# A hybrid decoder layer with retrieved experts: the first half's gates, merge and scores by two tiles at a time, and larger runs of the expert tables

## The chip, the core and the metric

The kernel runs on one core of one Trainium2 chip. The core has a matrix engine (TensorE, PE in the profile; its weight loads are PEld), a vector engine (VectorE, DVE), a scalar engine (ScalarE, ACT), GpSimd (POOL), which also issues the gathers, and SyncE (SP), which issues most other DMAs. All DMAs of the core run on 16 DMA engines. The metric is the device time of the launch in microseconds. Before the change it is 3426.83 us, the median of three executions.

## The reference

The layer takes `x` (1024 tokens of 1024 channels, float32). With `u` the normalised input it computes

```python
proj = u @ w_in                  # b_gate, c_gate, xc, q, k, v, g_conv, g_attn
y_conv = (b_gate * conv3(c_gate * xc)) @ w_conv_out
y_attn = merge3(dilated_window_attention(q, k, v)) @ w_attn_out    # 24 heads, 3 dilations
merged = sigmoid(g_conv + b0) * y_conv + sigmoid(g_attn + b1) * y_attn
h = x + merged @ w_out
u2 = rms_norm(h)
q = u2 @ w_query                 # 8 heads x 2 halves of 128
s = q . sub_keys                 # 128 scores for each half of each head
idx, gates = best 16 of the 256 sums of the top 16 of both halves
a = gelu(u2 . expert_down[idx])  # 8 x 16 = 128 of 16384 experts for each token
out = rms_norm(h + sum((gates * a) * expert_up[idx]))
```

The mixing is causal: the second half of the tokens reads keys, values and the convolution's carry of the first half.

## The kernel before

The tokens are two halves of 512, and tiles of 128. Matrix products run in fp32r with both sides split into a high and a low part, three matmuls for each pair of blocks (`mm3`, L175 to L178). `weights` (L161) loads 512 KB of a weight, casts the high part on ScalarE (L165) and subtracts it on DVE (L167, "a weight split" below); four buffers hold raw weights, two hold the split ones. `project` (L184) makes 24 matmuls from one weight and a block of activations, whose token columns are the moving side.

`mixer(half)` (L354) makes the projections, attention and convolution of a half, then its end: `gates` (L604; 16 projections and sigmoids), `merge` (L616; 8 products with `w_attn_out`, 8 with `w_conv_out`, each multiplied with its gate), `product` (L663; `w_out`, two columns halves, and the residual) and `tail` (L694; second norm, transposes, 16 projections with `w_query`, and the scores). The pair `SUBS[half]` says how the four tiles of a half are cut: the first number how many groups go through gates and merge, the second into how many parts a group is cut for product and tail. The first half has (1, 2): all four tiles through gates and merge with 512 columns, then product and tail for tiles 0 and 1, and for 2 and 3. While a tail waits for its norm, `AFTER` steps of what comes next are put ahead of it (L698).

The experts are computed in two ways. For tiles of the first half, `choose` (L756) finds the 16 best experts of each head on DVE, and `experts` (L861) gathers the rows of the chosen experts, 128 for each token, one row for each of the tile's 128 tokens at a time: POOL issues the gather of a 128x1024 block into one of four buffers, and DVE multiplies and sums it (L875, 512 times) or adds it into the result (L891, 384 times). For the second half and for tile 1's up products, `dense` (L900) goes through all 16384 experts: `hidden` (L909) computes gelu of the down products, 128 projections, `build` (L948) makes a table of gates by one-hot products (`g_d` in HBM), and then 32 steps follow. A step loads the stored hidden units (`fetch`, L920), reads its part of the table (`gg`, L984), multiplies and splits (`weigh`, L983), and runs 120 matmuls against the rows of `up` (L1063), whose splits are `uh` and `ul`. `STORED` = 27 of the 32 blocks of hidden units go through HBM; four (`HOLD`) stay in buffers, and one is computed within the loop (L1041).

What sets the order: each engine takes its instructions in one order that is fixed when the kernel is built. The builder's scheduler sees the instructions in the order of the program, in which the generators are interleaved by paces (`PACE_B`, `PACE_C`, `PACE_D`, L1108 to L1120), and may move a later one ahead when it takes an engine to be idle and the instruction ready. The experts' generator stands behind the first half in the program (L1103 to L1105). The pool of ten big buffers (`BIGS`, 16 KB of each partition) holds most activations, `gg`, `ga`, `hh` and `hl`.

Of the kernel before, what the change touches and what calls it, by code (L numbers as in the profile page):

```python
# [8 lines left out]
F32 = mybir.dt.float32  # L9
# [4 lines left out]
ALU = mybir.AluOpType  # L14
# [22 lines left out]
RATE_G = 0.8  # L37
STORED = 27
HOLD = 4
RAWS = 4  # L40
HILO = 2
SUBS = ((1, 2), (1, 1))
OBUF = 4
# [22 lines left out]
def hybrid_layer(ctx, tc, x, xT, pos, rotc, norm_mix, w_proj, w_v, conv_w, w_conv_out, w_attn_out,  # L66
                 gate_bias, w_out, norm_ffn, w_query, sub_keys, down, down_t, up, final_norm, out):
    nc = tc.nc
# [111 lines left out]
    def split(hi, lo, src):  # L180
        S.copy(hi, src)  # L181
        V.tensor_tensor(lo, src, hi.bitcast(F32), op=ALU.subtract)  # L182
# [717 lines left out]
    def dense():  # L900
# [47 lines left out]
        def build(srcs, c0):  # L948
# [5 lines left out]
                for c in range(c0, c0 + P // TC):  # L954
# [25 lines left out]
                    for w in range(4):  # L980
                        nc.sync.dma_start(g_d[c, :, 32 * w:32 * w + 32], stg[w])

        def weigh(q):  # L983
            gg = m8.tile([P, TH // TC, NB, TC], F32, tag="big", name="gg")  # L984
            nc.sync.dma_start(gg, g_d[:TH // TC, :, NB * q:NB * q + NB].rearrange("c j i t -> j c i t"))
            ga = gas.pop(q)
            hh, hl = bigr("hh"), bigr("hl")
            for ii in range(NB):
                v = ga[:, ii].rearrange("p (c t) -> p c t", t=TC)
                V.tensor_tensor(v, v, gg[:, :, ii], op=ALU.mult)  # L990
                split(hh[:, ii], hl[:, ii], ga[:, ii])
            parts = [(hh[:, :, tt * P:tt * P + P], hl[:, :, tt * P:tt * P + P]) for tt in range(4)]
# [41 lines left out]
        for n_q, q in enumerate(order):  # L1034
# [22 lines left out]
            for n in range(2):  # L1057
                uu = []
                whole = [bigr("uh_end"), bigr("ul_end")] if end and n else None
                for ii in range(0, NB, 2):  # L1060
                    raw = wp.tile([P, 2, TH], F32, tag="raw", bufs=RAWS, name="rawu")
                    r0 = (NB * q + ii) * P
                    nc.sync.dma_start(raw, up[r0:r0 + 2 * P, n * TH:n * TH + TH].rearrange("(a p) d -> p a d", a=2))  # L1063
                    if whole:
                        uh, ul = (t[:, ii:ii + 2] for t in whole)
                    else:
                        uh = up_p.tile([P, 2, TH], F32R, tag="uu", bufs=UPS, name="uh")
                        ul = up_p.tile([P, 2, TH], F32R, tag="uu", bufs=UPS, name="ul")
                    split(uh, ul, raw)
                    uu.append((uh, ul))  # L1070
# [105 lines left out]
```

## Time and profile before

| | |
|---|---|
| median of three executions | 3426.83 us (3426.28 to 3431.36) |
| the profiled execution | 3433.88 us |
| its span, first to last instruction | 3432.1 us |
| mean granted clock of TensorE | 0.984 |
| busy: TensorE, DVE, ScalarE, POOL | 3274.4, 2760.1, 1461.7, 1190.2 us |
| DMA | 948.08 MB, 276 GB/s in the mean |

A stretch of time is read by the engines' busy time in it: the one that is busy all the time sets its length, and where two are, the order in which each takes its work decides. Matmuls are pipelined, so the mean duration of one in a group is longer than the distance from one to the next; that distance is a stretch's time over its count. Small float32 products that aren't split (scores, transposes, table) show as two matmuls each.

### The profile page before, as it was taken

Reading aid. Unit: us, or ns where it says so; the run is one execution under the profiler, and the core shown is the slowest. Engines: PE = TensorE matmul, PEld = TensorE weight load, DVE = VectorE, ACT = ScalarE, POOL = GpSimd, SP = SyncE. Lnnn points to the kernel's source line nnn. Section 1 sums busy time; section 2 is a strip of 40 time slices with the busy share of each in tenths; the row PEclk is TensorE's granted clock in tenths of the full one; section 3 lists DMA queues with packets and bytes.
Section 4 is the critical chain, followed back from the end, with each engine's and each line's share of the span. In section 5 each row is a group of like instructions: output and inputs, shape, how many; then the busy total and the mean of one; then the engine's idle time right before and its main releaser. Section 6 shows DMA issues by size and latency. Waiting matters only on the chain.

```text
span 3432.1 us, 47074 instructions
## 1 busy us (share of the span) xinstructions
PE 3274.4 (95%) x15923; PEld 2685.0 (78%) x15923; DVE 2760.1 (80%) x5646; ACT 1461.7 (43%) x3271; POOL 1190.2 (35%) x944
## 2 busy tenths in 40 slices
PE   7999999999989999988999989999999999999998
PEld 6787888887767777767777878888877878787787
DVE  4333355689999889988999999998887878888887
ACT  3544444443334353333226777787632222222222
POOL 0000000014543345555434443464544334444342
PEclk9999999999989999989999999999999999999999
DMA  4233335668888678988889898999989989999895
GB/s 129 77 119 110 103 127 191 244 230 305 302 279 276 227 260 307 342 316 292 315 316 328 329 330 334 344 340 336 348 301 336 334 316 338 326 340 333 309 350 208
DMA packets 364307, 948.08 MB, mean 276 GB/s; under 512 B 33952, under 2 KB 127648, under 8 KB 356640
## 3 DMA queue, kind: packets, MB, share of 16 engines
q1 hardware_dynamic: 232016, 465.27, 38.9%
q0 software_dynamic: 132048, 479.78, 38.8%
q8 instruction: 126, 2.06, 0.2%
q14 instruction: 117, 0.96, 0.1%
HBM read 843.15 MB, written 95.49 MB: 273 GB/s over the span
## 4 chain that ended last, share of the span: by engine, by line
PE 32%; DVE 20%; DMA 14%; issue 11%; POOL 5%; ACT 1%; SPq 0%; DVEq 0%; POOLq 0%; ACTq 0%
DVE row L875 6%; PE ps L178 6%; PE ps L176 6%; PE ps L177 6%; DMA row<-in_down,idx 5%; DMA rowu<-in_up,idx 4%; DMA gg<-g_d 4%; DVE lo L167 3%; POOL row L873 3%; POOL rowu L889 2%; PE held L177 2%; PE held L178 2%; PE held L176 2%; DVE acc L891 1%; PE psg L975 1%
## 5 line engine op out<-in xcount | busy, mean ns | idle before, releaser
L873 POOL DMA_INDIRECT row<-in_down,idx x512 | 640.9, 1252 | 885.2 <-DVE a L875 465.6
L889 POOL DMA_INDIRECT rowu<-in_up,idx x384 | 525.8, 1369 | 621.1 <-DVE acc L891 499.0
L165 ACT CAST hi<-raw 128x1024 fp32r<-128x1024 f32 x368 | 387.6, 1053 | 746.0 <-PE ps L177 541.1
L875 DVE CUSTOM_DVE_ANT_0 row<-row,ut 128x1024 f32<-128x1024 f32 x512 | 618.8, 1215 | 79.2 <-DMA row<-in_down,idx 74.0
L167 DVE TENSOR_TENSOR lo<-raw,hi 128x1024 fp32r<-128x1024 f32 x368 | 448.1, 1218 | 247.9 <-ACT hi L165 238.6
L178 PE MATMUL ps<-vhi,lo 128*128 128x512 f32 (+1 forms) x1408 | 535.4, 382 | 33.5 <-DVE lo L167 33.4
L176 PE MATMUL ps<-vhi,hi 128*128 128x512 f32 (+1 forms) x1408 | 530.6, 377 | 10.8 <-ACT hi L165 6.7
L891 DVE SCALAR_TENSOR_TENSOR acc<-rowu,a,acc 128x1024 f32<-128x1024 f32 x384 | 491.2, 1279 | 59.7 <-DMA rowu<-in_up,idx 57.3
L177 PE MATMUL ps<-vlo,hi 128*128 128x512 f32 (+1 forms) x1408 | 528.9, 376 | 0.0
L178 PE MATMUL ps<-uhi,lo 128*128 128x512 f32 x1024 | 409.1, 400 | 4.2 <-DVE lo L167 4.2
L176 PE MATMUL ps<-uhi,hi 128*128 128x512 f32 x1024 | 407.6, 399 | 5.7 <-ACT uhi L181 3.1
L177 PE MATMUL ps<-ulo,hi 128*128 128x512 f32 x1024 | 409.1, 400 | 0.5 <-DVE ulo L182 0.5
L178 PEld LDWEIGHTS ps<-vhi,lo 128*128 128x128 f32 x1408 | 269.1, 191 | 87.4 <-DVE lo L167 44.4
L176 PEld LDWEIGHTS ps<-vhi,hi 128*128 128x128 f32 x1408 | 269.7, 192 | 58.9 <-ACT hi L165 10.9
L177 PEld LDWEIGHTS ps<-vlo,hi 128*128 128x128 f32 x1408 | 269.1, 191 | 45.1
L177 PE MATMUL held<-ul,hh 128*128 128x512 f32 x624 | 247.0, 396 | 11.1 <-DVE ul L182 10.9
L178 PE MATMUL held<-uh,hl 128*128 128x512 f32 x624 | 244.0, 392 | 2.5 <-DVE hl L182 2.5
L176 PEld LDWEIGHTS ps<-uhi,hi 128*128 128x128 f32 x1024 | 194.1, 190 | 52.1 <-ACT uhi L181 5.2
L176 PE MATMUL held<-uh,hh 128*128 128x512 f32 x624 | 233.3, 393 | 0.0
L178 PEld LDWEIGHTS ps<-uhi,lo 128*128 128x128 f32 x1024 | 194.3, 190 | 47.9 <-DVE lo L167 6.4
L177 PEld LDWEIGHTS ps<-ulo,hi 128*128 128x128 f32 x1024 | 194.1, 190 | 45.1 <-issue 3.0
L181 ACT CAST hh<-ga 128x512 fp32r<-128x512 f32 x128 | 71.4, 618 | 353.0 <-DVE ga L990 348.9
(347 smaller groups left out, 5947.8 us busy)
## 6 DMA issues: line engine op xcount, KB each, us to landing
raw<-in_w_proj SPq DMA_DIRECT2D x128, 512.0 KB
raw<-in_down_t SPq DMA_DIRECT2D x128, 512.0 KB
rawu<-in_up SPq DMA_DIRECT2D x128, 512.0 KB
g_d<-stg SPq DMA_DIRECT2D x80, 512.0 KB
gg<-g_d SPq DMA_DIRECT2D x32, 1024.0 KB
a_d<-ga SPq DMA_DIRECT2D x27, 1024.0 KB
ga<-a_d SPq DMA_DIRECT2D x27, 1024.0 KB
raw<-in_w_query SPq DMA_DIRECT2D x48, 512.0 KB
```

Of the source, the lines that this page charges most:

```text
L165: S.copy(hi, raw)
L167: V.tensor_tensor(lo, raw, hi.bitcast(F32), op=ALU.subtract)
L176: PE.matmul(ps, l[0], r[0], start=first, stop=False)
L177: PE.matmul(ps, l[0], r[1], start=False, stop=False)
L178: PE.matmul(ps, l[1], r[0], start=False, stop=last)
L181: S.copy(hi, src)
L873: G.indirect_dma_start(out=row, out_offset=None, in_=down, in_offset=bass.IndirectOffsetOnAxis(ap=idx[:, e:e + 1], axis=0))
L875: V.tensor_tensor_reduce(out=row, in0=row, in1=ut, scale=1.0, scalar=0.0, op0=ALU.mult, op1=ALU.add, accum_out=a[:, e:e + 1])
L889: G.indirect_dma_start(out=row, out_offset=None, in_=up, in_offset=bass.IndirectOffsetOnAxis(ap=idx[:, e:e + 1], axis=0))
L891: V.scalar_tensor_tensor(acc, row, a[:, e:e + 1], acc, op0=ALU.mult, op1=ALU.add)
L975: PE.matmul(ps[:, t], ob[:, t], oa[:, t], start=True, stop=True)
```

## The change

In the first half, `SUBS` becomes (2, 1): tiles 0 and 1 go through gates, merge, product and tail, then tiles 2 and 3. Gates and merge so run on 256 columns, and twice. Four gate projections of the second group stand ahead of the first tail, where the second product stood.

`weigh` reads the table for two steps at once: at an even step two transfers bring half of the tokens each, in runs of 1 KB where there were runs of 512 B, and both stay for the odd step. It multiplies and splits in pieces of 128x1024. For the pairs to be whole, `STORED` is 28, and no hidden block is computed within the loop. The rows of `up` come from a copy that is laid out ahead of the launch, so that each partition reads one run of 4 KB where it read two of 2 KB.

```diff
-STORED = 27
+STORED = 28
...
-SUBS = ((1, 2), (1, 1))
+SUBS = ((2, 1), (1, 1))
...
+        pairs = {}
+
         def weigh(q):
-            gg = m8.tile([P, TH // TC, NB, TC], F32, tag="big", name="gg")
-            nc.sync.dma_start(gg, g_d[:TH // TC, :, NB * q:NB * q + NB].rearrange("c j i t -> j c i t"))
+
+            c2 = TH // TC // 2
+            if q // 2 not in pairs:
+                both = []
+                for half in range(2):
+                    gg = m8.tile([P, c2, 2 * NB, TC], F32, tag="big", name="gg")
+                    i0 = 2 * NB * (q // 2)
+                    nc.sync.dma_start(gg, g_d[c2 * half:c2 * half + c2, :, i0:i0 + 2 * NB].rearrange("c j i t -> j c i t"))
+                    both.append(gg)
+                pairs[q // 2] = both
+            gg2 = pairs[q // 2]
             ga = gas.pop(q)
             hh, hl = bigr("hh"), bigr("hl")
-            for ii in range(NB):
-                v = ga[:, ii].rearrange("p (c t) -> p c t", t=TC)
-                V.tensor_tensor(v, v, gg[:, :, ii], op=ALU.mult)
-                split(hh[:, ii], hl[:, ii], ga[:, ii])
+            for half in range(2):
+                cols = slice(half * TH // 2, half * TH // 2 + TH // 2)
+                v = ga[:, :, cols]
+                g = gg2[half][:, :, NB * (q % 2):NB * (q % 2) + NB].rearrange("p c i t -> p i c t")
+                V.tensor_tensor(v.rearrange("p i (c t) -> p i c t", t=TC), v.rearrange("p i (c t) -> p i c t", t=TC), g,
+                                op=ALU.mult)
+                split(hh[:, :, cols], hl[:, :, cols], v)
...
-                    r0 = (NB * q + ii) * P
-                    nc.sync.dma_start(raw, up[r0:r0 + 2 * P, n * TH:n * TH + TH].rearrange("(a p) d -> p a d", a=2))
+                    nc.sync.dma_start(raw, up_s[(NB * q + ii) // 2, n])
...
+        "up_s": i["peer_up"][0].reshape(P // 2, 2, P, 2, TH).transpose(0, 3, 2, 1, 4),
```

The order of instructions changes with it. The first place is DVE's order where the first gathered rows stand. Before, they stand in the second tail, between the splits of `w_query`; the choice of tile 0 ends with L828, and L762 to L766 choose for tile 1:

```order
L826 SCALAR_TENSOR_TENSOR e_5667<-e_5667 128x128
L828 CAST idx<-e_5667 128x128
L762 MAX tv<-sv 128x8 x4
L763 MAX_INDEX ti<-tv,sv 128x8 x2
L167 TENSOR_TENSOR lo<-raw,hi 128x1024
L763 MAX_INDEX ti<-tv,sv 128x8 x2
L764 MATCH_REPLACE sv<-tv,sv 128x128 x4
L765 MAX tv<-sv 128x8 x2
L875 ISA row,a<-row,ut 128x1024
L875 ISA a 128x1
L765 MAX tv<-sv 128x8
L167 TENSOR_TENSOR lo<-raw,hi 128x1024
```

After, on the same engine, they stand in the merge of tiles 2 and 3, between the splits of `w_conv_out`; L631 multiplies the gate with the attention product, L649 with that of the convolution:

```order
L167 TENSOR_TENSOR lo<-raw,hi 128x1024
L631 TENSOR_TENSOR sg_4701<-sg_4701,ya 128x256
L764 MATCH_REPLACE sv<-tv,sv 128x128 x3
L875 ISA row,a<-row,ut 128x1024
L875 ISA a 128x1
L765 MAX tv<-sv 128x8 x4
L875 ISA row,a<-row,ut 128x1024
L875 ISA a 128x1
L167 TENSOR_TENSOR lo<-raw,hi 128x1024
L649 TENSOR_TENSOR sg_5868<-sg_5868,ys 128x256
L766 MAX_INDEX ti<-tv,sv 128x8 x4
L875 ISA row,a<-row,ut 128x1024
```

The row products have moved ahead of a merge's end, a product and a tail of the first half.

The second place is SP's order in the steps of `dense`, two steps of each kernel. Before, a step fetches `ga` and its table `gg`, then goes on with the rows of `up` (`rawu`) and tile 1's part of the table (`gx`):

```order
L922 DMA ga<-a_d 128x2048
L985 DMA gg<-g_d 128x16x128
L1063 DMA rawu<-in_up 128x2x512
L996 DMA gx<-g_d 128x4x128
L1063 DMA rawu<-in_up 128x2x512 x3
L922 DMA ga<-a_d 128x2048
L985 DMA gg<-g_d 128x16x128
L1063 DMA rawu<-in_up 128x2x512
L996 DMA gx<-g_d 128x4x128
L1063 DMA rawu<-in_up 128x2x512 x3
```

After, the two parts of a pair's table stand on both sides of three loads of `up`:

```order
L922 DMA ga<-a_d 128x2048
L1076 DMA rawu<-in_up_s 128x1024
L1010 DMA gx<-g_d 128x4x128
L922 DMA ga<-a_d 128x2048
L993 DMA gg<-g_d 128x8x256
L1076 DMA rawu<-in_up_s 128x1024 x3
L993 DMA gg<-g_d 128x8x256
L1076 DMA rawu<-in_up_s 128x1024
L1010 DMA gx<-g_d 128x4x128
L1076 DMA rawu<-in_up_s 128x1024 x3
```

The odd step has no table to read; the even step's second part is issued behind loads that wait for a raw buffer.

## Rows read from the trace of the kernel before

**Rows 1.** The page: busy us of each engine, and tenths in 40 slices.
```profile
PE 3274.4 (95%) x15923; PEld 2685.0 (78%) x15923; DVE 2760.1 (80%) x5646; ACT 1461.7 (43%) x3271; POOL 1190.2 (35%) x944
...
PE   7999999999989999988999989999999999999998
...
DVE  4333355689999889988999999998887878888887
```

**Rows 2.** Stretches: us, busy PE, PEld, DVE, ACT, POOL, clock, DMA share, GB/s.
```profile
500.00:628.00 128.00, 126.62 (x551) 102.53 (x551) 76.67 (x110) 65.33 (x90) 0.68 (x1) 1.00 0.59 202
628.00:776.00 148.00, 138.44 (x952) 127.30 (x952) 123.81 (x389) 68.48 (x139) 17.96 (x17) 0.95 0.68 237
776.00:1057.00 281.00, 258.09 (x1325) 207.54 (x1323) 267.48 (x851) 100.49 (x200) 133.63 (x121) 0.94 0.87 295
1057.00:1609.00 552.00, 517.68 (x2535) 417.43 (x2534) 484.02 (x964) 217.16 (x414) 254.35 (x203) 0.97 0.83 288
1609.00:1924.00 315.00, 292.79 (x1362) 238.02 (x1362) 302.61 (x853) 142.72 (x349) 134.74 (x112) 0.99 0.89 319
1924.00:2461.00 537.00, 521.05 (x2787) 446.45 (x2787) 506.48 (x955) 405.17 (x1281) 252.83 (x173) 0.98 0.91 336
2461.00:3432.00 971.00, 939.71 (x4067) 762.20 (x4066) 793.30 (x1049) 246.15 (x352) 394.06 (x307) 0.99 0.89 319
```

**Rows 3.** The same view: 512-column work alone, then mostly 256-column work.
```profile
560.00:595.00 35.00, 35.00 (x156) 29.01 (x155) 20.86 (x28) 13.54 (x19) 0.00 (x0) 1.00 0.31 103
655.00:690.00 35.00, 35.00 (x298) 35.00 (x297) 29.67 (x94) 17.34 (x44) 1.08 (x2) 1.00 0.65 209
```

**Rows 4.** Groups on DVE, 628 to 776 us: count, busy us, mean ns, idle before.
```profile
L167 DVE TENSOR_TENSOR lo<-raw,hi 128x1024 fp32r<-128x1024 f32 x36 | 43.9, 1219 | 15.0 <-ACT hi L165 14.9
L875 DVE CUSTOM_DVE_ANT_0 row<-row,ut 128x1024 f32<-128x1024 f32 x8 | 9.7, 1221 | 2.2 <-DMA row<-in_down,idx 2.1
L182 DVE TENSOR_TENSOR vlo<-pst,vhi 128x256 fp32r<-128x256 f32 x16 | 6.3, 416 | 0.3 <-ACT vhi L181 0.2
...
L765 DVE MAX8 tv<-s_t 128x8 f32<-128x128 f32 x16 | 4.6, 290 | 0.4
```

**Rows 5.** Groups of the whole span, by form.
```profile
L875 DVE CUSTOM_DVE_ANT_0 row<-row,ut 128x1024 f32<-128x1024 f32 x512 | 618.8, 1215 | 79.2 <-DMA row<-in_down,idx 74.0 <-issue 4.0 <-DMA ut<-u_d 0.9
...
L891 DVE SCALAR_TENSOR_TENSOR acc<-rowu,a,acc 128x1024 f32<-128x1024 f32 x384 | 491.2, 1279 | 59.7 <-DMA rowu<-in_up,idx 57.3
...
L167 DVE TENSOR_TENSOR lo<-raw,hi 128x1024 fp32r<-128x1024 f32 x368 | 448.1, 1218 | 247.9 <-ACT hi L165 238.6 <-DMA raw<-in_w_proj 4.2 <-PE pst L548 2.1
...
L165 ACT CAST hi<-raw 128x1024 fp32r<-128x1024 f32 x368 | 387.6, 1053 | 746.0 <-PE ps L177 541.1 <-issue 104.3 <-PE pv L178 43.6
...
L962 DVE TENSOR_TENSOR oa<-iota,sT 128x512 f32<-128x512 f32 x160 | 106.1, 682 | 2.4 <-issue 1.5 <-PE psg L975 0.9
...
L182 DVE TENSOR_TENSOR hl<-ga,hh 128x512 fp32r<-128x512 f32 x128 | 81.2, 687 | 1.7 <-PE held L177 1.0 <-ACT hh L181 0.7
...
L968 DVE TENSOR_TENSOR ob<-ob,sT 128x512 f32<-128x512 f32 x80 | 54.2, 682 | 1.7 <-ACT ob L967 1.7
```

**Rows 6.** Waits, 2491 us to the end: total us, times, longest; DVE's, then TensorE's.
```profile
DVE ga L990 <- DMA gg<-g_d: 73.3, 26, 8.4
...
PE held L177 <- DVE ul L182: 10.9, 9, 2.4
PE ps L176 <- ACT ga L913: 3.0, 1, 3.0
PE held L178 <- DVE hl L182: 2.5, 1, 2.5
PE psu L176 <- DVE rest L1089: 2.4, 4, 1.0
```

**Rows 7.** Chain that ended last, 2780 to 2900 us: start, us, what.
```profile
2803.84 16.12 DMA gg<-g_d
...
2836.50 9.39 DMA gg<-g_d
```

More of the change, by code (lines that the diff above doesn't have):

```diff
@@ L66, in hybrid_layer @@
 def hybrid_layer(ctx, tc, x, xT, pos, rotc, norm_mix, w_proj, w_v, conv_w, w_conv_out, w_attn_out,
-                 gate_bias, w_out, norm_ffn, w_query, sub_keys, down, down_t, up, final_norm, out):
+                 gate_bias, w_out, norm_ffn, w_query, sub_keys, down, down_t, up, up_s, final_norm, out):
     nc = tc.nc
```

## The prediction

> **What bounds the kernel now.** I read the page first. TensorE is busy for 3274.4 us of 3432.1, VectorE (DVE) for 2760.1, and the tenths show DVE at 3 to 6 in the first 8 slices of 40, hardly lower than TensorE from there on [rows 1]. So TensorE sets the pace, but for more than a thousand microseconds a second engine stands almost as high. Busy time by stage comes next, to see where; then the groups of instructions, for durations, and last the waits and the chain of the final stage. From 500 to 628 us (merging of the first half) TensorE is busy for 126.6 of 128 us and DVE for 76.7. From 628 to 776 (the two tails of the first half) it is 138.4 and 123.8 of 148; from 776 to 1057 it is 258.1 and 267.5 of 281: here DVE is at 95% and TensorE waits for it. From 1609 to 2461 (hidden units and table) both stand at 93 to 97%. From 2461 to the end (up products) TensorE has 939.7 of 971 and DVE only 793.3 [rows 2]. What fills DVE is the gathered expert rows: 512 products of 1.215 us (L875) and 384 sums of 1.279 (L891) [rows 5]. They may run anywhere once their indices are known; the order on DVE, fixed at build time, says where. A DVE microsecond after 2461 is nearly free, one between 628 and 1057 is paid by TensorE. The change has to be judged by where it puts these rows.
>
> **The change, part by part.** The profiled execution took 3433.9 us around its span of 3432.1, which is 7.1 us above the median of 3426.8; the sum is made on the former and carried to the latter.
>
> *Two tiles at a time (A).* 16 gate projections and 8 of `w_conv_out` (24 matmuls each) and 8 of `w_attn_out` (12 each) are 672 matmuls of 512 columns, and become 1344 of 256. A stretch of 512-column work alone made 156 matmuls in 35.00 us, 224 ns each; one of nearly only 256-column work made 298 in 35.00, 117 ns each, TensorE and its weight loads both full [rows 3]. Two halves cost 10 ns more than the whole: 672 x 10 ns = 7 us, and I add 1 us for the second start of the merge: **+8**. Bounds: 0 and, with a wait at each new stage, +14. The weights are also read and split twice: 24 x (1.05 us on ScalarE + 1.22 us on DVE) [rows 5]. The 16 of the gates fall into time with DVE at 60% [rows 2] and cost nothing; the 8 of `w_conv_out` come back below.
>
> The Trainium skill speaks against this part: "TensorE: Matmul & The Clock Gate", section "The mechanism", says that a weight load runs beside a matmul only when the row groups differ, which full 128-row loads never do. By the load and issue figures of that page (an estimate: 107 ns a load, 109 ns for 256 columns) the 672 pairs would cost 73 us instead of 7. The trace doesn't agree: 117 ns holds a load and a matmul together [rows 3], so the rule gets no chance of its own.
>
> *Gathered rows start earlier (T, M).* Tile 0 gets its scores after the first pair of tiles instead of after all four gates and merges, so its gathers start while the second pair's merge runs. I count on DVE's order, from the end: the second half and the hidden units need 236 weight splits (L167) in both kernels. Take the 36 splits before these. Before, they are the two tails, and 628 to 776 us holds just these: 36 splits and 8 row products [rows 4]. After, they are 8 of `w_conv_out`, 8 of `w_out`, 16 of `w_query` and 4 of the second half, and 55 row products stand among them. TensorE's work there is the same to a microsecond (16 `w_query` projections of 256 columns against 8 `w_conv_out` of 256 and 8 `w_out`, whose 12 matmuls of 512 columns are as many column steps). DVE's is not: 47 rows x 1.22 = 57 us; 8 attention splits (0.69 us each by `hl` of the same form [rows 5]), 24 merge products of 256 columns (0.42 by `vlo` [rows 4]) and two more splits of the stored y (1.22) add 18 us; 4 columns less of the choice of experts (5 operations of about 0.29 us each [rows 4]), two fewer normalised rows (1.28) and some small operations more nearly cancel. DVE had 123.8 us of work [rows 2] and gets about 198, in a stretch of 148 us. It takes its instructions in order, and with two buffers for split weights it can be no more than two weights ahead of TensorE, so the stretch cannot be shorter than DVE's work: **+50**. At the 95% of the next stretch it would be +60; if short operations overlap more than now, +40. What is queued behind a row are the splits, and TensorE waits for those.
>
> What comes back: these rows, and a part of the choice for tile 1, are out of the way later. Between split 236 and split 200 from the end stand 92 rows instead of 106: 14 x 1.22 = 17 us less, of which other work takes about 5, in a stretch where DVE is the limit: **-12** (0 to -20). From 200 to 128 stand 217 instead of 195 rows, but the choice is further on, about even; TensorE is the limit there at 94% [rows 2]: **-5** (-15 to +5).
>
> *The hidden units (H).* The row products are ahead, so the routing table is built earlier too: with 80 splits left, 64 of its 160 groups instead of 28. 36 groups more in the stretch now at 1609 to 1924 are 36 x (0.68 + 0.68) = 49 us of DVE [rows 5], which is busy for 302.6 of 315 there [rows 2]. They are missing from 1924 to 2461, but there TensorE is at 97% and gives back only its own share: 36 x 8 matmuls, about 0.11 us each by the 117 ns of [rows 3], some 32 us. +49 - 32, and 16 rows fewer in the whole: I take **+12** (-8 to +25).
>
> *The up products (U).* 39 rows fewer are left for this stage (from split 8 on), but DVE is not its limit. TensorE's waits are what could go: 10.9 and 2.5 us for `ul` and `hl`, 3.0 at the hidden block that leaves the loop, 2.4 for `rest` [rows 6]; the few us after the last matmul stay in any case. The pair read halves the waits of DVE for `gg` (73.3 us over 26 steps), and 1 KB and 4 KB runs instead of 512 B and 2 KB should shorten the transfers (9.4 and 16.1 us in two steps of the chain) [rows 6, 7]. No row shows such runs, so the bounds: -31 if every idle microsecond of TensorE (971 - 940) went, +20 by the wait of the second rival. The products of 128x1024 instead of 128x512 save DVE some 10 us, off the path. The hidden step that stood in this loop moves before it, at equal work. The waits of the list are nearest, and I take nearly all of them: **-18**.
>
> Sum: 8 + 50 - 12 - 5 + 12 - 18 = +35, which is 3469 for such an execution and **3462** at the median.
>
> **Rivals.** *The head start is a gain (20%).* The rows that DVE does early are rows that it need not do when it is at its limit, and all stages after the first half become TensorE's. For it: from 776 to 2461 TensorE has 1685 us and is busy for 1590; 95 us of idle time are to be had. Against it: from split 236 to split 8 the order after still has 577 rows, before 585; nearly the whole head start is handed on to the up products. If M and H return 30, 25 and 10 instead of 12, 5 and -12, and U returns 25, the sum is 8 + 45 - 30 - 25 - 10 - 25 = -37: 3390.
>
> *The pair read is a wait (12%).* Both parts of a pair's table, 2 MB, must land before an even step's product. On SP's queue the second part stands behind three loads of up rows, which wait for a free buffer; DVE stands at the second product with gathered rows and `ul` behind it. For it: 16.1 us for 1 MB in one step. Against it: two steps are 55 us. If each of 16 pairs holds DVE by the longest wait of now, 8.4 us [rows 6], that is 134 us instead of 73, and TensorE, which feels 11 of these 73, pays 9 more; a wait of 3 us in each pair that TensorE feels in full gives 48. Between the two I set U at +20 instead of -18: 3500. It decides once a wait exceeds DVE's slack, (971 - 793) / 32 = 6 us a step.
>
> *No change (10%).* T is paid, and the returns at their better ends take it back: 8 + 45 - 20 - 8 + 5 - 31 = -1, 3426.
>
> **Numbers.** The forecast has 58%; its own range, from the bounds of the terms, is 3435 to 3495. With the rivals I set 3405 to 3505: it leaves out the deeper half of the first and a little of the second. A median of three executions spreads over 5 us, so no change is within 0.2%, 7 us. Faster: the 20% of the first rival; same 10%; slower 70%.
>
> **What would show it.** For T: the 36 splits ahead of the second half's take about 198 us instead of 148, with DVE full, and TensorE waits at L178 for `lo`; its granted clock falls there. Were DVE full and the stretch at 160, the row count would be misread. For A: 117 ns a matmul in the gates. For H: TensorE idle moves from the end of the hidden stage to its beginning. For U: the last gathered row lies some 60 us or more before the end, and TensorE's waits for `ul` shrink; if they grow, the second rival has it. I am wrong if the second half and the hidden units together come out 60 us shorter than now.

## The result, and the profile after

The changed kernel takes 3479.44 us in the median of four executions (3476.86 to 3487.08), the kernel before 3426.56 on the same chip. The ratio is 1.0156, with a 95% interval of 1.0137 to 1.0176: slower by 53 us, where 35 were forecast. The profiled execution took 3480.45 us, with a span of 3478.7 and a mean clock of 0.978, against 3433.88, 3432.1 and 0.984.

The page of the changed kernel, busy times and tenths, to be read against [rows 1]:

```profile
PE 3296.8 (95%) x16595; PEld 2733.7 (79%) x16595; DVE 2790.3 (80%) x5582; ACT 1501.5 (43%) x3283; POOL 1254.5 (36%) x944
...
PE   7999989977989999889999998999999999999998
...
DVE  4333476899999889888999999998678888888864
```

TensorE now falls to 7 in the 9th and 10th slices, where it stood at 9 before, while DVE stands at 9 there. At the end DVE falls to 6 and 4: its rows run out before TensorE is done.

The two kernels do the same work for the second half, the hidden units and the up products, so both spans can be cut by the weight splits still to come on DVE (272, 236, ... of L167). First the stretches of the changed kernel (length, busy PE, PEld, DVE, ACT, POOL, clock, DMA share, GB/s), which begin at 332 splits left (the point where 308 were left before) and end at 272, 236, 200, 128, 80, 8 and the end:

```profile
429.70:659.70 230.00, 213.88 (x1566) 202.35 (x1567) 170.79 (x401) 127.75 (x223) 2.31 (x4) 0.96 0.64 216
659.70:854.30 194.60, 152.41 (x928) 134.46 (x927) 184.38 (x501) 75.28 (x125) 82.48 (x68) 0.89 0.87 313
854.30:1126.00 271.70, 257.61 (x1381) 207.72 (x1380) 259.30 (x825) 107.55 (x216) 115.17 (x105) 0.96 0.83 278
1126.00:1675.80 549.80, 515.49 (x2479) 414.31 (x2477) 473.88 (x813) 208.36 (x399) 284.98 (x221) 0.97 0.87 307
1675.80:2025.40 349.60, 327.94 (x1657) 272.84 (x1658) 342.05 (x907) 220.19 (x656) 146.54 (x116) 0.99 0.88 320
2025.40:2533.00 507.60, 487.49 (x2506) 412.92 (x2506) 452.71 (x830) 328.22 (x978) 243.01 (x156) 0.99 0.88 324
2533.00:3478.70 945.70, 932.03 (x4053) 763.16 (x4051) 738.09 (x881) 245.43 (x280) 378.04 (x267) 0.99 0.83 304
```

The rows of before are in [rows 2], except the first, which it needs too:

```profile
429.90:628.00 198.10, 196.72 (x867) 160.22 (x868) 113.36 (x158) 92.73 (x129) 0.68 (x1) 1.00 0.52 175
```

Subtracted one by one: the first half's gates and merge (A) +32, the 36 splits after them (T) 194.6 against 148.0, **+47**; the second half (M) -9 and -2; the hidden units and the table (H) +34 and -29; the up products (U) -26. The sum is +47 of span, between two single executions; the medians differ by 53. T is the largest term, as forecast. Its groups on DVE show why (count, busy us, mean ns, idle before them):

```profile
L875 DVE CUSTOM_DVE_ANT_0 row<-row,ut 128x1024 f32<-128x1024 f32 x55 | 66.5, 1212 | 7.3 <-DMA row<-in_down,idx 7.3
L167 DVE TENSOR_TENSOR lo<-raw,hi 128x1024 fp32r<-128x1024 f32 x37 | 44.8, 1213 | 0.4 <-ACT hi L165 0.4
```

All 55 counted rows are there, and the splits have lost their idle time: 15.0 us for 36 in [rows 4], 0.4 now. DVE hardly waits for a weight any more; the weight waits for DVE. One such wait in order of time, first on DVE (start, us, instruction), then on TensorE:

```profile
715.50 1.20 DVE L875 CUSTOM_DVE_ANT_0 row<-row,ut 128x1024 f32<-128x1024 f32 x1
...
717.49 1.21 DVE L182 TENSOR_TENSOR ulo<-rawx,uhi 128x1024 fp32r<-128x1024 f32 x1
718.62 0.41 DVE L650 TENSOR_TENSOR sg<-sg,sg 128x256 f32<-128x256 f32 x1
718.96 1.21 DVE L875 CUSTOM_DVE_ANT_0 row<-row,ut 128x1024 f32<-128x1024 f32 x1
...
720.10 1.22 DVE L167 TENSOR_TENSOR lo<-raw,hi 128x1024 fp32r<-128x1024 f32 x1
```
```profile
721.37 0.58 PE L178 MATMUL ps<-yhi,lo 128*128 128x256 f32 x1 [4.96 <-DVE lo L167]
```

Two rows, a split of the second half's input and small products of the merge stand ahead of the split of a weight of `w_conv_out`; TensorE starts 0.05 us after it has ended, having stood for 4.96 us. It pays twice: around this wait the granted clock is at 1.2 GHz, from 718 to 725 us, and 0.89 in the mean of the stretch, against 0.95 in [rows 2]. TensorE is idle for 42 us of this stretch (194.6 - 152.4), 10 before; its largest waits there are all for DVE (total us, times, longest):

```profile
PE ps L178 <- DVE lo L167: 12.9, 10, 5.0
PE pst L716 <- DVE vlo L182: 7.8, 2, 4.7
PE po L177 <- DVE lo L167: 6.9, 3, 3.4
```

In the up products TensorE's waits of [rows 6], 10.9 us for `ul` at their head, have gone but for these two (total us, times, longest):

```profile
PE ps L178 <- DVE lo L167: 2.1, 1, 2.1
PE held L178 <- DVE hl L182: 2.1, 1, 2.1
```

The last gathered row ends 143 us before the span does (3335.5 us), where it was 34 (3397.8).

### The profile page after: what moved, and what is told of

It is laid out like the page before. It is cut to its first block, busy times and chain, and to the rows that moved or that the text cites. A ratio compares the mean times of both kernels' runs of the same rounds, so it can differ in the third digit from the quotient of the medians.

```text
span 3478.7 us, 48512 instructions
## 1 busy us (share of the span) xinstructions
PE 3296.8 (95%) x16595; PEld 2733.7 (79%) x16595; DVE 2790.3 (80%) x5582; ACT 1501.5 (43%) x3283; POOL 1254.5 (36%) x944
## 4 chain that ended last, share of the span: by engine, by line
PE 49%; DVE 16%; DMA 11%; issue 5%; POOL 2%; ACT 2%; SPq 0%; DVEq 0%; POOLq 0%; ACTq 0%
PE ps L178 6%; PE ps L176 6%; PE ps L177 6%; PE held L177 5%; PE held L176 5%; PE held L178 5%; DVE row L875 4%; DMA row<-in_down,idx 4%; PE psu L177 3%; PE psu L176 3%; PE psu L178 3%; DVE lo L167 3%; PE psg L975 2%; DMA rowu<-in_up,idx 2%; DMA g_d<-stg 2%
## 5 line engine op out<-in xcount | busy, mean ns | idle before, releaser
L873 POOL DMA_INDIRECT row<-in_down,idx x512 | 670.9, 1310 | 869.2 <-DVE a L875 474.9
L889 POOL DMA_INDIRECT rowu<-in_up,idx x384 | 559.9, 1458 | 584.2 <-DVE acc L891 436.3
L167 DVE TENSOR_TENSOR lo<-raw,hi 128x1024 fp32r<-128x1024 f32 x392 | 477.3, 1218 | 251.8 <-ACT hi L165 239.9
L178 PE MATMUL ps<-vhi,lo 128*128 128x512 f32 (+1 forms) x1408 | 533.9, 381 | 28.0 <-DVE lo L167 27.7
L176 PE MATMUL ps<-vhi,hi 128*128 128x512 f32 (+1 forms) x1408 | 531.7, 378 | 11.4 <-ACT hi L165 11.4
L891 DVE SCALAR_TENSOR_TENSOR acc<-rowu,a,acc 128x1024 f32<-128x1024 f32 x384 | 491.4, 1280 | 45.5 <-DMA rowu<-in_up,idx 42.7
L176 PE MATMUL ps<-uhi,hi 128*128 128x512 f32 (+1 forms) x1152 | 431.1, 375 | 10.0 <-ACT hi L165 7.2
L178 PE MATMUL ps<-uhi,lo 128*128 128x512 f32 (+1 forms) x1152 | 430.8, 374 | 7.3 <-DVE lo L167 7.3
L177 PE MATMUL ps<-ulo,hi 128*128 128x512 f32 (+1 forms) x1152 | 431.6, 375 | 0.5 <-DVE ulo L182 0.5
L178 PEld LDWEIGHTS ps<-vhi,lo 128*128 128x128 f32 x1408 | 269.1, 191 | 80.7 <-DVE lo L167 37.3
L176 PEld LDWEIGHTS ps<-uhi,hi 128*128 128x128 f32 x1152 | 219.7, 191 | 52.0 <-ACT hi L165 9.2
L178 PEld LDWEIGHTS ps<-uhi,lo 128*128 128x128 f32 x1152 | 220.2, 191 | 46.9 <-DVE lo L167 10.6
L177 PEld LDWEIGHTS ps<-ulo,hi 128*128 128x128 f32 x1152 | 220.1, 191 | 40.0 <-issue 3.5
L178 PE MATMUL held<-uh,hl 128*128 128x512 f32 x624 | 244.4, 392 | 2.1 <-DVE hl L182 2.1
L181 ACT CAST uh<-rawu 128x1024 fp32r<-128x1024 f32 x126 | 131.8, 1049 | 218.0 <-PE psu L178 166.1
```

The source lines that it names most:

```text
L167: V.tensor_tensor(lo, raw, hi.bitcast(F32), op=ALU.subtract)
L176: PE.matmul(ps, l[0], r[0], start=first, stop=False)
L177: PE.matmul(ps, l[0], r[1], start=False, stop=False)
L178: PE.matmul(ps, l[1], r[0], start=False, stop=last)
L873: G.indirect_dma_start(out=row, out_offset=None, in_=down, in_offset=bass.IndirectOffsetOnAxis(ap=idx[:, e:e + 1], axis=0))
L889: G.indirect_dma_start(out=row, out_offset=None, in_=up, in_offset=bass.IndirectOffsetOnAxis(ap=idx[:, e:e + 1], axis=0))
```

## The experiments

The cut of each kernel at the same splits, from its trace, in us (T is between 272 and 236 splits left, H between 128 and 8):

| kernel | median | to 272 | T | 236 to 200 | 200 to 128 | H | 8 to the end |
|---|---|---|---|---|---|---|---|
| before | 3426.6 | 628.0 | 148.1 | 281.0 | 551.9 | 851.9 | 971.2 |
| changed | 3479.4 | 659.7 | 194.6 | 271.7 | 549.8 | 857.3 | 945.6 |
| 1, reads without the cut | 3394.3 | 626.6 | 150.3 | 279.4 | 547.3 | 852.9 | 939.5 |
| 2, cut alone | 3494.2 | 656.8 | 194.8 | 272.2 | 546.2 | 861.3 | 961.4 |
| 3, 4 KB rows alone | 3418.2 | 626.5 | 148.8 | 278.2 | 548.4 | 851.4 | 969.5 |
| 4, pairs alone | 3396.0 | 627.9 | 148.2 | 276.9 | 550.0 | 845.8 | 940.6 |
| 5, changed, rows held | 3464.3 | 655.5 | 165.0 | 269.9 | 547.8 | 878.5 | 942.7 |
| 6, changed, third buffer | 3467.1 | 659.7 | 183.5 | 278.3 | 547.5 | 854.5 | 941.3 |
| 7, no cut, third buffer | 3415.5 | 627.6 | 146.6 | 283.1 | 554.9 | 870.6 | 939.1 |
| 8, no cut, program order | 3411.6 | 627.1 | 146.2 | 266.0 | 546.1 | 826.0 | 998.1 |
| 9, changed, prepare spread | 3473.7 | 651.4 | 185.6 | 275.1 | 546.1 | 877.9 | 943.7 |
| 10, no cut, program order 2 | 3416.4 | 627.5 | 144.0 | 271.0 | 555.7 | 878.1 | 938.5 |
| 11, pairs in 512 B runs | 3402.4 | 627.8 | 145.6 | 279.3 | 546.9 | 854.4 | 942.4 |

The medians of the experiments are over 6 or 12 executions, the columns from one profiled execution each; the kernel before was timed again beside each set and came to 3426 to 3432. How far single executions of one order scatter can be read from the table: before, 1, 3, 4 and 11 have the same order on DVE up to its last 40 instructions or so ahead of 8 splits left, and their columns differ by 1.5, 4.7, 4.1, 5.0 and 8.6 us; the changed kernel, 2 and 5 have the same order up to 272 splits left and differ by 4.2. A difference in a column that is smaller than this says nothing.

**1 to 4: which part does what.** Experiment 1 is the changed kernel with

```diff
-SUBS = ((2, 1), (1, 1))
+SUBS = ((1, 2), (1, 1))
```

> The changed kernel with SUBS set back to (1, 2) for the first half: the table read for two steps at once, the 4 KB rows of up and STORED = 28 alone. The order on DVE is that of the kernel before up to the last 8 weight splits. Theory 1 (the 25 us that the up products of the changed kernel won come from the larger reads): everything up to the last 8 splits as before, the up products 20 to 25 us shorter, 3402 to 3410 us. Theory 2 (they come from the 39 gathered rows that were done earlier): no gain here, 3420 to 3430. Theory 3 (the pair read is a wait that the head start of the rows only hid): the up products grow, over 3432. By theory 1 all of the loss of the changed kernel is that of the two-tile cut.

Experiment 2 is the kernel before with the opposite edit:

```diff
-SUBS = ((1, 2), (1, 1))
+SUBS = ((2, 1), (1, 1))
```

> The kernel before with SUBS = (2, 1) for the first half and nothing else. Theory 1: the cut costs what the changed kernel lost plus what its reads won, 53 + 25 = 78 us: 3500 to 3508 us, with 30 us in the merge of the first half and 45 in the stretch of the 36 splits ahead of the second half's, as in the changed kernel, and the up products no shorter than before. Theory 2 (the rows done earlier shorten the up products): 3475 to 3485, the up products 20 us shorter than before though the reads are the old ones.

Experiment 3 is the kernel before with this alone, and the copy `up_s` beside it:

```diff
-                    r0 = (NB * q + ii) * P
-                    nc.sync.dma_start(raw, up[r0:r0 + 2 * P, n * TH:n * TH + TH].rearrange("(a p) d -> p a d", a=2))
+                    nc.sync.dma_start(raw, up_s[(NB * q + ii) // 2, n])
```

> The kernel before with the 4 KB rows of up alone. TensorE waits for ul and hl in 13 us of the up products, and these come after a product with the table, not after the up rows. Theory 1a (the table read is what gains): 3422 to 3427 us, no change. Theory 1b (the runs of the up rows gain): 3405 to 3412, shorter transfers leave the queue to the table. The 4 KB transfers themselves should take less time on the DMA engines in either case: fewer packets, the same bytes.

Experiment 4 is experiment 1 with that edit undone, so that the new `weigh` and `STORED = 28` are alone:

```diff
-                    nc.sync.dma_start(raw, up_s[(NB * q + ii) // 2, n])
+                    r0 = (NB * q + ii) * P
+                    nc.sync.dma_start(raw, up[r0:r0 + 2 * P, n * TH:n * TH + TH].rearrange("(a p) d -> p a d", a=2))
```

> The kernel before with the table read for two steps at once and STORED = 28, the rows of up read as before in 2 KB runs. Theory 1a (the table read is what gains): 3405 to 3412 us, with most of the 13 us that TensorE waits for ul and hl gone. Theory 1b (the up rows' runs gain): 3420 to 3430. Theory 3 (the pair read alone is a wait): over 3432.

Measured: 3394.25 (ratio 0.990, interval 0.9878 to 0.9921), 3494.15 (1.0188, 1.0166 to 1.021), 3418.22 (0.9969, 0.9955 to 0.9984) and 3396.03 us (0.9907, 0.9883 to 0.9931). The changed kernel joins a gain of 32 us with a loss of 68. The gain is that of the table's pairs; the 4 KB rows take off 8 us when alone, and the 2 by which experiment 1 lies below 4 are within the spread of either. Experiments 1 and 4 gained 8 and 9 us more than their theories allowed, 2 lost 6 less, and 3 lies between its two; its transfers took a little less of the DMA engines, as expected: 44.3% of the up products' stage for SP's queue instead of 45.5, with the same bytes. In the up products the two parts don't add: the reads take off 31 us, the cut 10, both together 26. The stretches from 8 splits left, of experiments 1 and 2 (columns as above):

```profile
2456.40:3395.90 939.50, 930.09 (x4068) 762.63 (x4066) 786.53 (x923) 246.69 (x289) 440.74 (x309) 1.00 0.91 331
```
```profile
2531.00:3492.70 961.70, 935.20 (x4049) 760.69 (x4047) 743.67 (x1008) 244.50 (x342) 338.90 (x266) 0.99 0.83 297
```

With the pair read TensorE is busy for all but 9 us, which lie behind its last matmul, with 787 us of DVE work, 48 more than the changed kernel has there. What bounds this stage is then TensorE's 930 us, and rows done ahead of it are worth nothing. With the old reads DVE still makes TensorE wait, and fewer rows do help, by 10 us. What changed on DVE is the wait for the table (total us, times, longest), in the kernel with pairs alone; before it was 73.3 in 26 waits [rows 6]:

```profile
DVE ga L1003 <- DMA gg<-g_d: 38.1, 21, 6.1
```

**11: the runs, or the fetching for two?** In experiment 4 a transfer now brings both steps in 1 KB runs; here two are still issued together, but one for each step, in 512 B runs as before:

```diff
-                for half in range(2):
-                    gg = m8.tile([P, c2, 2 * NB, TC], F32, tag="big", name="gg")
-                    i0 = 2 * NB * (q // 2)
-                    nc.sync.dma_start(gg, g_d[c2 * half:c2 * half + c2, :, i0:i0 + 2 * NB].rearrange("c j i t -> j c i t"))
+                for step in range(2):
+                    gg = m8.tile([P, TH // TC, NB, TC], F32, tag="big", name="gg")
+                    i0 = 2 * NB * (q // 2) + NB * step
+                    nc.sync.dma_start(gg, g_d[:TH // TC, :, i0:i0 + NB].rearrange("c j i t -> j c i t"))
```

> The kernel of the fourth experiment (pair read, old up rows; 3396 us), with the table of two steps still fetched together at the even step, in two transfers of 1 MB, but one for each step, in the old runs of 512 B instead of 1 KB. The order of every engine is the same but for these transfers. Theory 1 (the gain comes from fetching for two steps at once: VectorE meets a table that is not there yet in every second step only): 3390 to 3402 us. Theory 2 (it comes from the runs of 1 KB, whose transfers land in 9 instead of 12.5 us): most of the gain goes, 3412 to 3428, and VectorE waits for gg again for 60 us or more.

It took 3402.44 us (0.9914, 0.9895 to 0.9933), 30 less than the kernel before in the same set, as experiment 4 did in its own. The stretch of its up products, and DVE's wait for the table there:

```profile
2454.00:3396.30 942.30, 930.63 (x4067) 763.08 (x4066) 784.81 (x923) 241.55 (x288) 436.87 (x309) 1.00 0.93 330
```
```profile
DVE ga L1003 <- DMA gg<-g_d: 45.7, 16, 5.7
```

Theory 1 holds: the gain is there without the longer runs. What stands beside the fetch in both 4 and 11 was not tried apart: the products in pieces of 128x1024 and `STORED = 28`, which takes a hidden block out of the loop. What speaks for the fetch is DVE's wait for the table: 38 and 46 us in these two instead of 73.

A transfer of 1 MB landed in 9.4 us in the median here (for the 13 of 32 whose landing the trace has) and in 9.2 in the changed kernel (8 of 32), 12.5 in experiment 2, which reads the same 512 B runs step by step (13 of 32). The Trainium skill, "DMA: Bandwidth & Descriptors", section "Specifications", gives 512 B as the least size that moves at line rate; the first two medians don't speak against it.

**5: the head start of the rows.** The row products of tile 0 may not stand on DVE ahead of the last split of the first half (`held_back` is taken at the last `w_query` weight):

```diff
-                V.tensor_tensor_reduce(out=row, in0=row, in1=ut, scale=1.0, scalar=0.0, op0=ALU.mult,
-                                       op1=ALU.add, accum_out=a[:, e:e + 1])
+                with tc.issue_after(held_back[0].ins):
+                    V.tensor_tensor_reduce(out=row, in0=row, in1=ut, scale=1.0, scalar=0.0, op0=ALU.mult,
+                                           op1=ALU.add, accum_out=a[:, e:e + 1])
```

> The changed kernel, but the row products of tile 0 (L875) may not stand on DVE ahead of the last split of w_query of the first half's second tail. 0 instead of 55 rows then stand among the 36 splits ahead of the second half's, and 105 instead of 92 in the next 36. Theory 1 (the head start of the rows costs what DVE needs for them): that stretch falls from 195 us to 150 to 160; the next one grows from 272 by the 13 rows, 10 to 16 us, since DVE is its limit; the up products stay at 940 to 950. In the whole 3440 to 3465 us against 3479, and still above the kernel before by the first half's merge. Theory 2 (the 256-column projections themselves, which hold a split weight for half as long, make the stretch long): it stays above 180, and the whole at 3475 or more.

3464.33 us (1.0109, 1.0087 to 1.0132). T fell to 165.0:

```profile
655.50:820.60 165.10, 145.42 (x939) 130.48 (x938) 134.34 (x450) 75.67 (x127) 11.11 (x14) 0.95 0.63 206
```

Without a row DVE has 134 us of work here instead of 184, and the stretch loses 30 us. That is theory 1, short of its range: 17 us are left over the 148 of before, with DVE at 81% only. Theory 2 may have a part of T as well, but that isn't shown, since the room did not stay empty: by summed durations the choice of experts (L756 to L828 of the changed kernel) takes 83 us of DVE here, 66 in the changed kernel and 68 before. The next stretch did not grow by the 13 rows that came into it:

```profile
820.60:1090.50 269.90, 254.32 (x1336) 205.99 (x1335) 255.84 (x770) 102.50 (x204) 131.15 (x116) 0.96 0.88 295
```

The choice that had moved out of it made up for them: 79 us there instead of 97. The hidden units did grow, by 21 us. In the whole the head start cost 15 us (3479.4 - 3464.3), not 30.

**6, 7 and 9: why the gates and the merge are longer.** TensorE's own work between 430 and 660 us is 213.88 us less 8.5 that the lower clock took (17 us at 1.2 GHz; the row shows 0.96), about 205, and was 197: +9, as forecast. The other 23 us of A are 16 idle (230 - 214; 1.4 before) and these 8.5. Experiments 2 and 5, whose order is the same up to here, reach 272 splits left at 656.8 and 655.5, so A is +28 to +32. Experiment 6 gives the high parts a third buffer (those of `w_attn_out` too, in the same way):

```diff
-GATES = 4
+GATES = 2
...
-        hi = wp.tile([P, n, D // n], F32R, tag="hi", bufs=HILO, name="hi")
+        hi = wp.tile([P, n, D // n], F32R, tag="hi", bufs=HILO + 1, name="hi")
```

> The changed kernel with three buffers instead of two for the high parts of split weights (paid for with GATES = 2 instead of 4, buffers of the expert choice, which has not begun in the gates). Theory 1 (in the gates and merges of 256 columns TensorE is through a weight in 24 x 117 ns = 2.8 us, and the next one can only be cast, 1.05 us, and subtracted, 1.22 us, into a freed pair of buffers in 2.3 us, so that any other instruction of ScalarE or DVE in between lets TensorE wait): with a third buffer the cast runs ahead, TensorE's waits for hi in the first half's gates and merge go, and the point of 272 splits left comes 10 to 20 us earlier than the 660 us of the changed kernel. The 36 splits after it stay at 185 to 195 us, since DVE is full there. In the whole 3455 to 3470. Theory 2 (DVE has too much work in the gates and merges as well): 660 stays within 5 us. Theory 3 (the 256-column matmuls cost it all): 660 stays too, and TensorE has no waits there to lose.

3467.08 us (1.0113, 1.009 to 1.0136), but the point of 272 splits left stayed at 659.7: theory 1 falls for A. T lost 11 us, as DVE's work there did (173.4 instead of 184.4): in this order 48 rows stand there instead of 55.

```profile
659.70:843.20 183.50, 147.16 (x915) 131.22 (x914) 173.40 (x478) 75.54 (x125) 70.51 (x60) 0.90 0.87 312
```

With the buffer free a cast could still meet the next thing in line. The longest such wait, on ScalarE, then SP's queue and TensorE of this kernel (start, us, instruction, idle time before it):

```profile
495.98 1.04 ACT L165 CAST hi<-raw 128x1024 fp32r<-128x1024 f32 x1 [6.58 <-DMA raw<-in_w_proj]
```
```profile
487.68 1.66 SPq L315 DMA_DIRECT2D u_d<-rawx  x2
491.06 0.33 SPq L163 DMA_DIRECT2D raw<-in_w_proj  x1
491.48 0.41 SPq L315 DMA_DIRECT2D u_d<-rawx  x1
```
```profile
497.07 0.58 PE L176 MATMUL ps<-uhi,hi 128*128 128x256 f32 x1 [8.19 <-ACT hi L165]
```

The load of the gate's weight stands on SP behind stores (`u_d<-rawx`) of the second half's scaled input, is issued at 491.06 and its cast starts 4.9 us later; TensorE stood for 8.2 us. These stores belong to `prepare`, of which a step stands ahead of each gate from the seventh on. In the changed kernel ScalarE shows the same neighbour, a square of `prepare` that waits for its input, with the cast of a weight right behind it, for which TensorE waits 1.9 us:

```profile
459.55 0.63 ACT L231 ACTIVATE sq<-rawx 128x512 f32<-128x512 f32 x1 [2.78 <-DMA rawx<-in_xT]
460.09 1.03 ACT L165 CAST hi<-raw 128x1024 fp32r<-128x1024 f32 x1
```

So experiment 9 spreads `prepare` over the gates of both groups:

```diff
-            for _ in second:
-                pass
+            if n_f + 1 == len(fronts):
+                for _ in second:
+                    pass
...
-                if 8 * (1 - j) + c >= AT_P:
+                if 8 * (1 - j) + c >= AT_P and c % 2 == 0:
```

> The changed kernel, with the ten steps of the second half's input norm and angles (prepare: squares, sums, scaled inputs, and loads of x that take raw buffers), which stand one by one ahead of gates 7 to 16 of tiles 0 and 1, put ahead of every second of these gates in both groups of tiles, five in each. Theory 1 (the first half's gates are longer than 256-column matmuls make them, because the work of a half on ScalarE and DVE that stood beside 16 gates of 512 columns now stands beside 16 of half the time, and in its in-order queue the casts of the weights wait behind it): TensorE's 16 us of waits and 8 us of lower clock between 430 and 660 us fall to a half, and the point of 272 splits left comes 8 to 15 us earlier than 660. Theory 2 (the rest is the attention's normalisation and the shorter use of a weight, not this work): 660 within 4 us. Either way the 36 splits after it stay at 185 to 200 us.

3473.7 us (1.0134, 1.0114 to 1.0153); 272 splits left at 651.4, 8 us earlier:

```profile
429.30:651.40 222.10, 210.54 (x1576) 199.65 (x1577) 166.13 (x386) 127.60 (x222) 2.31 (x4) 0.98 0.66 216
```

TensorE's idle time went from 16 to 12 us and the clock from 0.96 to 0.98. In the first group, to 308 splits left, the gain is 14 us (95.3 instead of 109.3, and 107.8 in 2 and 5); the second group, which now has five of the steps, gives 6 back. First the two groups of the changed kernel, then those of experiment 9:

```profile
429.70:539.00 109.30, 98.25 (x715) 93.40 (x716) 78.72 (x120) 63.91 (x98) 0.00 (x0) 0.94 0.63 213
539.00:659.70 120.70, 115.63 (x854) 108.95 (x853) 92.07 (x281) 63.84 (x127) 2.31 (x4) 0.99 0.64 218
```
```profile
429.30:524.70 95.40, 92.93 (x715) 89.34 (x716) 69.40 (x105) 57.24 (x91) 0.00 (x0) 0.98 0.60 189
524.70:651.40 126.70, 117.62 (x863) 110.31 (x862) 96.73 (x282) 70.37 (x132) 2.31 (x4) 0.99 0.71 236
```

Theory 1 holds at its lower end: 8 of A's 32 us are this neighbourhood in the queues, 4 if the 655.5 of experiment 5 is the measure; the two groups, which move by more than the scatter and against each other, show it more clearly than the sum does. Of the 24 that are left in experiment 9 TensorE's own work is 10. In the whole it is 6 us faster than the changed kernel, and the two intervals overlap.

Experiment 7 is experiment 1 with the same:

```diff
-GATES = 4
+GATES = 2
...
-        hi = wp.tile([P, n, D // n], F32R, tag="hi", bufs=HILO, name="hi")
+        hi = wp.tile([P, n, D // n], F32R, tag="hi", bufs=HILO + 1, name="hi")
```

> The reads of the changed kernel without the cut (as in the first experiment, 3394 us), with the third buffer for high parts and GATES = 2. With 512 columns a weight lasts TensorE 24 x 224 ns = 5.4 us, three more than the cast and the subtraction need; the tails, with 256 columns, have the short time too. Theory 1: little to win up to the first tail, the tails (36 splits, 150 us) a few us shorter, 3380 to 3394. Theory 2 (fewer buffers for the choice cost more): 3396 to 3410.

3415.54 us (0.9963, 0.9947 to 0.9978), 21 slower than experiment 1. T is 146.6 us, among the 144 to 150 of all kernels without the cut, so the third buffer shows no gain there; the hidden units took 18 more. The total lies above the ranges of both theories, on the side of theory 2; that it is GATES, and not the other order of rows and table in the hidden units, isn't shown.

**8 and 10: where should the rows be?** In experiment 1 every row, product or sum, is held behind the weight split that stands ahead of it in the program (`latest`, taken at L167); in 8 with PACE_B = 2.2, in 10 with PACE_C = 2.0 and RATE_G = 0.9:

```diff
+                with tc.issue_after(latest[0].ins):
-                V.scalar_tensor_tensor(acc, row, a[:, e:e + 1], acc, op0=ALU.mult, op1=ALU.add)
+                    V.scalar_tensor_tensor(acc, row, a[:, e:e + 1], acc, op0=ALU.mult, op1=ALU.add)
```

> The reads of the changed kernel without the cut (3394 us), and every gathered row, product or sum, stays on DVE behind the weight split that stands ahead of it in the program, with PACE_B = 2.2: 93 instead of 106 rows stand in the first 36 splits of the second half, where DVE is at 95%, and 330 instead of 305 beside the up products, where it had 787 us of work in 939. Theory 1 (a DVE microsecond in the second half is paid by TensorE, one beside the up products is free): the first 36 splits of the second half 10 to 15 us shorter than 279, the up products 939 to 945, 3370 to 3390 us. Theory 2 (beside the up products it is paid as well, in waits for ul and hl): up products over 955, 3395 or more.

> The kernel in which every gathered row stays behind the weight split ahead of it in the program, with PACE_B = 2.0, PACE_C = 2.0 and RATE_G = 0.9, so that 100 rows instead of 93 stand in the second half's first 36 splits, 176 instead of 202 sums and none instead of 18 groups of the table beside the up products. In the earlier such run the stages up to the up products came out 45 us shorter than without the hold, and the up products 59 us longer: a wait of 14 us at their start, behind the table's end, and 24 us of lower clock at the end, when the last rows were late. Theory 1 (these two were the price of rows and groups put off, and go with them): up products 938 to 950, the whole 3375 to 3395 us. Theory 2 (what is put back costs in the hidden stage what it saves in the up products): the hidden stage 850 or more, 3395 to 3410.

3411.62 (0.996, 0.9944 to 0.9977) and 3416.37 us (0.9962, 0.9948 to 0.9975): both lose against experiment 1, on the side of theory 2 each time; the second lies 6 us above its range. In 8, 13 rows fewer made the first 36 splits of the second half 13 us shorter, and the hidden units won 27; the up products gave back 59. First its stretches from 236 splits left to 200, the hidden units and the up products, then the start of the last, where TensorE stood behind the last groups of the table (the cast that makes `hh` came behind copies that waited 11.4 us for a store of it):

```profile
773.30:1039.30 266.00, 255.22 (x1345) 206.30 (x1344) 254.95 (x840) 101.22 (x203) 126.59 (x109) 0.97 0.84 279
1585.40:2411.40 826.00, 796.50 (x3997) 664.77 (x3996) 773.27 (x1774) 507.69 (x1469) 350.27 (x274) 0.99 0.91 328
...
2411.40:3409.50 998.10, 953.69 (x4228) 783.54 (x4227) 836.89 (x984) 287.55 (x449) 470.95 (x332) 0.98 0.91 330
```

```profile
2500.78 0.80 PE L178 MATMUL held<-uh,hh 128*128 128x512 f32 x1 [14.26 <-ACT hh L183]
```

TensorE is busy for 24 us more in these up products than in experiment 1, with 160 matmuls more (144 of them the 18 groups of the table that were put off) and a lower clock, and is without work for 44 us instead of 9. In 10 the up products are as in experiment 1 (938.5), but the hidden units are 25 us longer.

## Why the prediction was right, and where it was not

**The direction and the case were right**: T is paid, and the returns don't cover it. 3479 lies in the forecast's own range. That it comes within 17 us of 3462 is partly luck: of the span's 12 us beyond the forecast (47 for 35) A alone is 24 and M's smaller returns are 6; T, H and U were 3, 7 and 8 better than forecast and hide a part of it.

**T** was to be 198 instead of 148, with DVE full, waits at L178 for `lo` and a falling clock. It is 194.6, DVE is at 184.4 (95%), and waits and clock are there. That the size fits is again partly luck, for two errors cancel. The working added up durations: 75 us more on DVE. By durations it is 74 (142 before, 217 after), but they overlap: a row product is listed with 1.21 us, and the next instruction starts 1.14 us after it (the median of the 465 behind which DVE didn't wait). DVE's busy time so grew by 61, not 75. On the other side DVE was idle for 10 us, 7.3 of them for gathered rows. The prediction had both as bounds, +40 and +60.

Nor is it all DVE's surplus, as the working had it: experiment 5 shows 30 for the rows, net of the choice that took their place, and 17 that remain at DVE 81%. They are 10 us more of idle time of TensorE than in the stretch of before, 5 of TensorE's own work and 2 of lower clock. The step "TensorE's work there is the same to a microsecond" missed the 5, and the reasoning by DVE's total the 10: below a full DVE I had put no wait at all.

**A is the step that failed**: +8 was forecast, 0 to 14 the bounds, +32 is measured. The sentence on TensorE's own cost held (+9). What failed is "the 16 of the gates fall into time with DVE at 60% and cost nothing". A busy share says nothing of the order in a queue: the casts, the subtractions and the loads of weights, twice as dense now, stand in line behind `prepare`, on ScalarE and on SP, and a late one stops TensorE, as in the two waits shown. Experiment 9 moved that work away and took back 8; the third buffer of 6 took back nothing. About 14 us of idle time and lower clock are left in A without a cause shown.

**M** came out as forecast in its first stretch (-9 for -12), and for the reason given: by summed durations DVE's rows take 118 us there instead of 137, and 8 of other work come in. Experiment 5, with 13 rows more, is as short only because it has 18 us less of the choice there. The second (-2 for -5) is within the scatter.

**H** was +12 and is +5, less than the scatter of the column, in the shape forecast: +34 early, -29 late, for +49 and -32. The sign named for it did not show: TensorE's idle time early is 22 us in both kernels, late 20 instead of 16. The early part is longer because both engines have more work in it, TensorE 35 us (328 instead of 293) and DVE 39.

**U** was -18 with bounds of -31 and +20, and is -26. The wait named, DVE's for `gg`, is the one that shrank; the longer runs are not its cause, and the fetch for two steps is what remains (with the pieces and `STORED`, as said). Experiments 1 and 4 come to the bound of -31, "if every idle microsecond of TensorE went", but not by that road: 9 us of idle time stay behind the last matmul, 22 went, and the rest is TensorE's busy time, 930 us instead of 940, which the bound took as fixed. Some 3 of these 10 are the clock (0.99 before, 1.00); the others are not explained. That the 39 rows are off the limit there is right with the pair read, and 10 us wrong without it.

**The rivals.** The pair read is no wait: alone it is worth 30 us. The head start is no gain: holding it back wins 15. "No change" asked for returns of 54 us (20 + 8 - 5 + 31); they were 32 (9 + 2 - 5 + 26). What stays open is why the hidden units are 18 to 26 us longer in experiments 5, 7, 9 and 10 than in 1, whose matmuls there are the same within 20 of 4150, and whose rows are nearly as late as those of 5: TensorE's waits and its lower clock make it up, and the order of rows and table differs in each. The 15 us of experiment 5 are net of this.

## What to carry to other kernels

Halving the width of a projection costs TensorE little, but it halves the time in which the next weight must be loaded, cast and subtracted, so first read the queues that feed it, instruction by instruction, and not their busy shares. Work that is brought forward is a gain only where the engine that does it has room then and is a limit later; here 61 us of DVE's time went into a stretch in which it had 24 of room. Test the parts of a mixed change apart: the reads alone, without the cut, make 3394 us, 1% faster than the kernel before and, with the pairs alone (3396), the fastest version found here.

## What the runs showed of the hardware

Where the table is read for two steps at once, a 1 MB read lands no later in runs of 512 B than of 1 KB: 9.4 and 9.2 us in the median, of 13 and 8 reads, against 12.5 (13 reads) where the same 512 B runs are read step by step. Why the single ones land later wasn't tried apart. The durations of DVE's instructions overlap: a row product is listed with 1.21 us, the next instruction starts after 1.14, and the accumulator read of 0.08 us that follows each product starts together with the instruction behind it, in all 512 cases of the changed kernel. Counts of work by summed durations are too high by this: 217 us for 184 of busy time in T.
